# Sorted experts' weights as whole 8 KB rows of one expert, a gather buffer allocated a group later, and the residual added in the fourth group

## The chip, the core and the metric

One core of a Trainium2 chip runs the whole program. The metric is the device time of one execution in microseconds. The kernel before took 951.91 us (median of 3 runs, 950.81 to 952.39). The profiled execution took 952.46 us, of which 950.6 us lie between its first and its last instruction.

## What is computed

A trunk of two post-norm layers over 256 tokens of 1024 channels. Each layer has a token mixer (three attentions and their projections, which the change does not touch) and a mixture of 16 experts, of which every token uses two of one group of four:

```
x = layer_norm(x, ln_in_g, ln_in_b)
for l in range(2):
    mix = token_mixer(x, ...)
    x = layer_norm(ALPHA * x + mix, ln1_g[l], ln1_b[l])
    ffn = grouped_moe(x, router_w, router_bias, w_gate[l], w_up[l], w_down[l])
    x = layer_norm(ALPHA * x + ffn, ln2_g[l], ln2_b[l])

# grouped_moe, with combine (256 x 16) zero but for the two experts chosen per token
for e in range(16):
    hid = silu(t @ w_gate[e]) * (t @ w_up[e])       # w_gate, w_up: 1024 x 512
    out = out + combine[:, e:e+1] * (hid @ w_down[e])   # w_down: 512 x 1024
```

All weights are float32, 6 MB for an expert in a layer, and each is read once: 96 MB of experts per layer.

## The kernel before

**Order of the work.** TensorE, GpSimd and the DMA queue of SyncE (SP) run in the order in which the program is written; VectorE and ScalarE are ordered by a scheduler. A first pass over the program, without instructions, plans when buffers are held and dropped; a second pass writes it.

**Buffers.** SBUF holds 25 slots of 8 KB per partition (`NS = 25`). Activations take some (x, xT, the split copies xh and xl, y, the gather buffer B), and all weights go through the others: a weight tile is one slot, 1 MB, 2048 floats on each of 128 partitions. `weight(i)` asks for load number i, `drop(i)` gives its slot back, and after each drop `pump()` (L267) issues as many further loads as the plan leaves slots for. A load is a DMA on SP's queue. It waits for the last reader of its slot.

**The expert groups.** `build_stream` lists the loads of a layer: first the mixer's, then the experts in seven groups p = 0 to 6. Groups 0 and 1 are experts 0 to 3, two each. The other 12 experts are sorted on the chip by their number of tokens, so that which expert is loaded is known only when the sorting (`sort`, L1270) is done: the four smallest form group 2 ("four"), and groups 3 to 6 hold two each. Each group has the loads of w_gate, w_up and w_down, each in two halves h.

**What a weight tile holds before.** A half h of a weight is 128 rows (partitions) of 2048 floats. A tile of the kernel before holds one half of that half (`i`, 1024 floats, 4 KB per row) for two experts side by side. A sorted tile is loaded by two DMAs of 512 KB, one for each expert, since their numbers come from registers (L243 to 245). The four's half h is four tiles, a pair's is two.

**What a group computes.** In `moe`, tokens gathered for the experts of a group (xg) are multiplied with gate and up (L1488): for the four 128-row blocks rr of half h, one matmul of each expert in turn; each expert's outputs stand on their own rows of the PSUM bank. `done` (L1580) drops a tile after every second rr. Then follow Silu and product, the scatter of the group before (`scatter`, L1425 to 1429: its outputs are added to the sums R in PSUM by one-hot matrices), four transposes (L1512), and w_down (L1535), whose outputs go to y. The very last tile of the last group's w_down is loaded in four DMAs of 256 KB, so that its last piece is small.

**What else the change touches.** `seeds` (L1420) opens the sums R with the residual: eight matmuls of the split x with the identity, in group 1. `gather` (L1366) makes xg for the next four or the next two pairs; for pairs it needs a second buffer, `self.B`, which is allocated in the first call, in group 1.

Of the kernel before, what the change touches and what calls it, by code (L numbers as in the profile page):

```python
# [17 lines left out]
L, T, D, E, FF = 2, 256, 1024, 16, 512  # L18
KC = D // 128
# [111 lines left out]
class Kernel:  # L131
# [49 lines left out]
    def build_stream(self):  # L181
        self.loads = []
        self.units = []
        for l in range(L):
            off = 0
            for g, n, w in GROUPS:
                k = 0
                while k < n:
                    m = min(PER_SLOT[g], n - k)
                    sid = len(self.loads)  # L190
                    self.loads.append(("mix", l, off, m * w))
                    j = 0
                    while j < m:
                        u = min(PER_UNIT[g], m - j)
                        self.units.append(dict(l=l, g=g, k=k + j, n=u, w=w, slot=sid, o=j * w,
                                               last=(j + u == m)))
                        j += u
                    k += m
                    off += m * w
            self.moe_base = getattr(self, "moe_base", {})  # L200


            self.groups = [(0, 1), (2, 3)]
            if self.general:
                self.groups += [(e, e + 1) for e in range(4, E, 2)]
            else:
                self.groups += [tuple(range(E - QUAD, E))] + [(e, e + 1) for e in range(FIXED, E - QUAD, 2)]
            for p, g in enumerate(self.groups):
                self.moe_base[l, p] = len(self.loads)
                for nm in ("w_gate", "w_up", "w_down"):  # L210
                    for h in range(2):
                        for i in range(2):
                            for e in range(0, len(g), 2):
                                self.loads.append((nm, l, g[e], h, i))
        self.li = 0
        self.order, self.numbers = {}, {}
        self.wt = {}
        self.ui = 0
        self.si = 0
        self.split_tiles = {}  # L220
        self.used = []

    def load_next(self):
        d = self.loads[self.li]
        if d[0] == "mix":
            _, l, off, n = d
            t = self.S.new([128, 2048], F32, "w", weight=True)
            m = 672 if off == 0 else n
            for i in range(0, n, m):
                self.nc.sync.dma_start(t[:, i:i + m], self.a["w1"][l, :, off + i:off + i + m])  # L230
        else:
            nm, l, e, h, i = d
            t = self.S.new([128, 2048], F32, "w", weight=True)
            t2 = t.rearrange("p (i n) -> p i n", i=2)
            dma, w = self.nc.sync.dma_start, self.a[nm]
            if (nm, e, h) == ("w_gate", 0, 0):

                dma(t2, w[l, i, h].rearrange("i p n -> p i n"))
            elif self.sorted(d):

                n = 2 if nm == "w_down" and (e, h, i) == (self.groups[-1][0], 1, 1) else 1
                for k in range(n):
                    o = slice(k * 1024 // n, (k + 1) * 1024 // n)  # L243
                    for j in range(2):
                        dma(t2[:, j, o], w[l, bass.ds(self.number(l, e + j), 1), h, i, :, o].rearrange("e p n -> p (e n)"))
            else:
                dma(t2, w[l, e:e + 2, h, i].rearrange("e p n -> p e n"))
        self.wt[self.li] = t
        self.li += 1
        if self.li == self.LATE:  # L250
            self.late_loads()

    def sorted(self, d):

# [74 lines left out]
    WARM0 = (6, 0)  # L329
    LATE = 4  # L330
    DENSE = (1, 1, 5)
    BT = 2

    def unit(self, keep=False):
# [1079 lines left out]


    def seeds(self):
        self.R = [[self.psum([128, 512], "ab"[t]) for _ in range(2)] for t in range(2)]
# [7 lines left out]
    def scatter(self, oht, ys, t, js=(0, 1)):  # L1425
        lt = oht[:, t * 128:(t + 1) * 128]
        for j in js:
            for i in range(2):
                self.nc.tensor.matmul(self.R[t][j], lt, ys[:, i, j], start=False, stop=True, skip_group_check=True)

    def moe(self, l, last_layer):
        nc = self.nc
# [7 lines left out]
        p = 2  # L1440
# [4 lines left out]
        self.xg, self.bk, self.oh, self.ohr = {}, {}, {}, {}  # L1445
# [6 lines left out]
        first = self.gather_pair(0)  # L1452
# [3 lines left out]
        late = None  # L1456
        for p, es in enumerate(G):
            xg = self.xg[p]
            n = len(es)
# [19 lines left out]
            for which, h in ((0, 0), (1, 0), (0, 1), (1, 1)) if p == 0 else ((0, 0), (0, 1), (1, 0), (1, 1)):  # L1479
                ps = (pg, pu)[which]  # L1480
                known = p == 0 and which == 0 and h == 0
                i0 = wi + (4 * which + 2 * h) * n // 2
                for rr in range(4):
                    r = 4 * h + rr
# [1 line left out]
                        nc.tensor.matmul(ps[:64], self.oh[0][:, rr, 0], self.G[:, rr], start=rr == 0, stop=False)  # L1486
                    for e in range(int(known), n):
                        nc.tensor.matmul(ps[e * w:(e + 1) * w], xg[:, r, e * w:(e + 1) * w],  # L1488
                                         self.block(i0, n, rr, e, known), start=r == 0, stop=r == KC - 1)
                    self.done(i0, n, rr, known)  # L1490
# [22 lines left out]
            nc.scalar.activation(ht, ph, AF.Copy)  # L1513
            next(seeds, None)
            if p == 1:
                self.scatter(*late, 0)
            if late:
                self.scatter(*late, 1)
            if last:
                self.tail_rows()  # L1520
            self.steps(gath, ga[1])
# [8 lines left out]
                ysum = self.ts[:, 8:10]  # L1530
            for j in range(2):
                i0 = wi + (8 + 2 * j) * n // 2
                for c in range(4):
                    for e in range(n):
                        nc.tensor.matmul(py[j][e * w:(e + 1) * w], ht[:, c, e * w:(e + 1) * w],  # L1535
                                         self.block(i0, n, c, e), start=c == 0, stop=c == 3)
                    self.done(i0, n, c)
                self.pump()
                if j == 0:
                    self.steps(gath, 4)  # L1540
# [29 lines left out]
        if last_layer:  # L1570
            self.rest()

    def block(self, i, n, k, e, known=False):

        if known:
# [4 lines left out]
    def done(self, i, n, k, known=False):  # L1580

        if known and k == 3:
            self.drop(i + 1)
            self.pump()
        elif not known and k % 2:
            for j in range(n // 2):
                self.drop(i + k // 2 * n // 2 + j)
                self.pump()

    def steps(self, gen, n):  # L1590
        for _ in range(n):
# [76 lines left out]
    def overflow(self, l, hs):  # L1668
# [15 lines left out]
            nc.vector.tensor_tensor(xT[:, r], xT[:, r], pb[:, 2:].rearrange("p t n -> p (t n)"), op=OP.add)  # L1684

        def part(nm, e, h):
            nc.sync.dma_start(w[h].rearrange("p (i n) -> p i n", i=2), self.a[nm][l, e, h].rearrange("i p n -> p i n"))

        for e in range(E):
            for t in range(2):  # L1690
# [100 lines left out]
def _pack(x):  # L1791
# [51 lines left out]
    ke = lambda w: w.reshape(L, E, 2, 2, 2, 128, FF).transpose(0, 1, 2, 3, 5, 4, 6).reshape(L, E, 2, 2, 128, 1024)  # L1843
    kd = lambda w: w.reshape(L, E, 2, 2, 128, 2, 512).transpose(0, 1, 5, 2, 4, 3, 6).reshape(L, E, 2, 2, 128, 1024)
# [20 lines left out]
```

## Time and profile before

| | us |
|---|---|
| median of 3 runs | 951.91 (950.81 to 952.39) |
| profiled execution | 952.46 |
| its span, first to last instruction | 950.6 |
| TensorE busy in it | 905.7 (95%) |
| granted TensorE clock | 0.996 of full speed |

The two layers look alike. In the first, the mixer ends and routing begins near 251 us, the experts' matmuls run from 272.8 to 473.0 us, and the next layer's mixer begins at 479.6 us; in the second the experts run from 736.3 to 936.1 us. The busy share of TensorE stays near nine tenths in every stage, in the later expert groups too, where the waits named in the timeline are waits for weights: a matmul's busy time there includes standing behind one whose weights are late. So the share alone does not tell what binds; the chain that ended last and the releasers of the waits do.

### The profile page before, as it was taken

To read this page: it belongs to the slowest core of one execution; us is meant where nothing else is said; L and a number is where in the kernel's file an instruction comes from. 1 tells how busy PE (TensorE), PEld (TensorE's weight loads), DVE (VectorE), ACT (ScalarE), POOL (GpSimd) and SP (SyncE) were. 2 spreads that over 40 slices of the span, in tenths; PEclk is the share of its full clock that TensorE was granted. 3 is DMA by queue.
4 is the path that set the end of the run, shared out by engine and by line. 5 is a ranking of instruction groups with operands and counts; after the bars stand their busy time and mean duration, and the time that the engine had idled before them with its cause. 6 is when DMAs were issued, how large, how long until landed. Compare 5 with 4: busy or idle time off the path is not lost.

```text
span 950.6 us, 15321 instructions
## 1 busy us (share of the span) xinstructions
PE 905.7 (95%) x5835; PEld 624.5 (66%) x5835; DVE 425.1 (45%) x754; ACT 368.2 (39%) x724; POOL 295.5 (31%) x217
## 2 busy tenths in 40 slices
PE   5999999999999999999989999999999999999995
PEld 4999989899754543433379989889985443444322
DVE  6686666648741111100177765684686211111004
ACT  4586646563412111011256766566433111111003
POOL 4359646563300100010071977465622010000000
PEclk9999999999999999999999999999999999999998
DMA  9941263748879999999994407363978899999994
GB/s 342 377 157 67 79 255 110 290 166 322 309 273 351 410 404 409 409 401 409 405 415 188 175 2 263 114 250 112 347 264 331 317 364 390 409 409 409 401 410 153
DMA packets 68842, 277.22 MB, mean 292 GB/s; under 512 B 7428, under 2 KB 8068, under 8 KB 62852
## 3 DMA queue, kind: packets, MB, share of 16 engines
q1 hardware_dynamic: 68056, 272.88, 74.6%
q10 hardware_dynamic: 576, 3.15, 0.9%
q8 instruction: 48, 0.79, 0.3%
q14 instruction: 34, 0.28, 0.1%
q0 software_dynamic: 128, 0.13, 0.0%
HBM read 275.08 MB, written 1.05 MB: 290 GB/s over the span
## 4 chain that ended last, share of the span: by engine, by line
PE 60%; DMA 27%; DVE 6%; ACT 3%; POOL 2%; issue 2%; SPq 1%; ACTq 0%; POOLq 0%; DVEq 0%
DMA w<-in_w_up_dram 9%; DMA w<-in_w_gate_dram 9%; DMA w<-in_w_down_dram 9%; PE psa L736 8%; PE psa L738 7%; PE psa L737 7%; PE psa L1488 7%; PE pss L1535 5%; PE psa L157 2%; PE psa L1014 2%; PE psb L992 2%; PE psa L158 2%; PE psa L159 2%; PE psa L1346 2%; PE pss L931 1%
## 5 line engine op out<-in xcount | busy, mean ns | idle before, releaser
L301 POOL TENSOR_TENSOR whl<-w,whl 128x1024 fp32r<-128x1024 f32 (+1 forms) x83 | 193.4, 2345 | 189.4 <-ACT whl L297 113.1
L297 ACT ACTIVATE whl<-w 128x1024 fp32r<-128x1024 f32 (+2 forms) x146 | 138.6, 967 | 70.1 <-PE psa L738 29.1
L1488 PE MATMUL psa<-w,xT 128*64 128x512 f32 (+1 forms) x752 | 145.7, 595 | 3.0 <-DMA w<-in_w_up_dram 3.0
L736 PE MATMUL psa<-xTh,whl 128*128 128x256 f32 x480 | 138.3, 288 | 1.6 <-DVE oT L1017 1.4
L737 PE MATMUL psa<-xTl,whl 128*128 128x256 f32 x480 | 135.7, 283 | 0.0
L738 PE MATMUL psa<-xTh,whl 128*128 128x256 f32 x480 | 135.6, 283 | 0.0
L1488 PEld LDWEIGHTS psa<-w,xT 128*64 128x64 f32 (+1 forms) x752 | 45.7, 127 | 99.7 <-issue 86.0
L1535 PE MATMUL pss<-w,xT 128*64 128x512 f32 (+1 forms) x512 | 100.1, 595 | 0.0
L736 PEld LDWEIGHTS psa<-xTh,whl 128*128 128x128 f32 x480 | 91.8, 191 | 8.5 <-issue 6.2
L1499 DVE TENSOR_TENSOR xT<-xT,psa 128x512 f32<-128x512 f32 x14 | 9.6, 687 | 195.3 <-PE psa L1488 195.3
L738 PEld LDWEIGHTS psa<-xTh,whl 128*128 128x128 f32 x480 | 91.9, 191 | 0.0
L737 PEld LDWEIGHTS psa<-xTl,whl 128*128 128x128 f32 x480 | 91.9, 191 | 0.0
L1488 PE MATMUL psa<-w,xg 128*64 128x512 f32 x256 | 72.8, 605 | 4.4 <-DMA w<-in_w_up_dram 2.7
L301 DVE TENSOR_TENSOR whl<-w,whl 128x768 fp32r<-128x768 f32 (+2 forms) x63 | 67.3, 1089 | 14.2 <-ACT whl L297 13.7
L1535 PEld LDWEIGHTS pss<-w,xT 128*64 128x64 f32 (+1 forms) x512 | 32.0, 130 | 54.3 <-issue 50.4
L477 POOL MEMSET lngb<- 128x2048 f32 x2 | 3.6, 1806 | 200.1 <-DMA w<-in_w_gate_dram 100.1
L1488 PEld LDWEIGHTS psa<-w,xg 128*64 128x64 f32 x256 | 22.0, 136 | 54.5 <-issue 23.6
L736 PE MATMUL psa<-oT,whl 128*128 128x256 f32 x192 | 55.3, 288 | 0.0
L1552 DVE SCALAR_TENSOR_TENSOR y<-pss,ws,y 128x512 fp32r<-128x512 f32 x26 | 19.5, 750 | 79.0 <-ACT y L1551 74.0
L737 PE MATMUL psa<-oT,whl 128*128 128x256 f32 x192 | 54.3, 283 | 0.0
L738 PE MATMUL psa<-oT,whl 128*128 128x256 f32 x192 | 54.3, 283 | 0.0
L1551 ACT ACTIVATE y<-pss,ws 128x512 fp32r<-128x512 f32 x26 | 17.8, 686 | 77.3 <-PE pss L1535 64.1
(346 smaller groups left out, 1669.4 us busy)
## 6 DMA issues: line engine op xcount, KB each, us to landing
w<-in_w_gate_dram SPq DMA_DIRECT2D x96, 512.0 KB, 10.1
w<-in_w_up_dram SPq DMA_DIRECT2D x96, 512.0 KB, 10.1
w<-in_w_dram SPq DMA_DIRECT2D x46, 1024.0 KB, 7.2
w<-in_w_down_dram SPq DMA_DIRECT2D x92, 512.0 KB, 10.1
w<-in_w_gate_dram SPq DMA_DIRECT2D x16, 1024.0 KB, 5.0
w<-in_w_up_dram SPq DMA_DIRECT2D x16, 1024.0 KB, 7.7
w<-in_w_down_dram SPq DMA_DIRECT2D x16, 1024.0 KB, 7.4
w<-in_w_dram SPq DMA_DIRECT2D x18, 768.0 KB, 13.3
```

Of the source, the lines that this page charges most:

```text
L157: mm(out, lh, rh, start=start, stop=False, skip_group_check=skip)
L158: mm(out, ll, rh, start=False, stop=False, skip_group_check=skip)
L159: mm(out, lh, rl, start=False, stop=stop, skip_group_check=skip)
L297: self.nc.scalar.activation(hi[:, :n], raw, AF.Copy)
L301: e.tensor_tensor(lo[:, :n], raw, hi[:, :n].bitcast(F32), op=OP.subtract)
L736: mm(out, wh, xh, start=start, stop=False, skip_group_check=True)
L737: mm(out, wh, xl, start=False, stop=False, skip_group_check=True)
L738: mm(out, wl, xh, start=False, stop=stop, skip_group_check=True)
L992: nc.tensor.transpose(ps[:, kc, t * 128:(t + 1) * 128], P[:, t, j, kc * 128:(kc + 1) * 128], self.ident)
L1488: nc.tensor.matmul(ps[e * w:(e + 1) * w], xg[:, r, e * w:(e + 1) * w], self.block(i0, n, rr, e, known), start=r == 0, stop=r == KC - 1)
L1535: nc.tensor.matmul(py[j][e * w:(e + 1) * w], ht[:, c, e * w:(e + 1) * w], self.block(i0, n, c, e), start=c == 0, stop=c == 3)
L1552: nc.vector.scalar_tensor_tensor(ys[:, 1, j], py[j], ws, ys[:, 0, j].bitcast(F32), op0=OP.mult, op1=OP.subtract)
```

## The change

1. Weights of the experts lie in HBM as [layer, expert, half h, 128, 2048] instead of [layer, expert, h, i, 128, 1024] (an arrangement made on the host). For groups 2 to 6, a weight tile is now one expert's whole half h: one DMA of 1 MB with 8 KB rows. Only the last half of w_down in the last group keeps the old form (`whole`). Groups 0 and 1 keep it too, but for the first half of their w_gate, which held one expert per tile already and is now read in 8 KB rows.
2. `block` and `done` follow: a matmul of expert e reads the tile of e, and the tiles of a half are all dropped after its fourth block rr.
3. `self.B` is allocated by the first gather for pairs, in group 2.
4. R is opened by the first scatter, in group 1 (`first`), and the residual's eight matmuls are added in group 3 (`SEED = 3`).

```diff
@@ build_stream
                 for nm in ("w_gate", "w_up", "w_down"):
                     for h in range(2):
-                        for i in range(2):
-                            for e in range(0, len(g), 2):
-                                self.loads.append((nm, l, g[e], h, i))
+                        if self.whole(nm, p, h):
+                            self.loads += [(nm, l, e, h, None) for e in g]
+                        else:
+                            self.loads += [(nm, l, g[0], h, i) for i in range(2)]
@@ load_next
-            if (nm, e, h) == ("w_gate", 0, 0):
-
-                dma(t2, w[l, i, h].rearrange("i p n -> p i n"))
+            one = lambda e: w[l, bass.ds(self.number(l, e), 1), h].rearrange("e p n -> p (e n)") if self.sorted(d) else w[l, e, h]
+            if i is None:
+                dma(t, one(e))
             elif self.sorted(d):
...
                     for j in range(2):
-                        dma(t2[:, j, o], w[l, bass.ds(self.number(l, e + j), 1), h, i, :, o].rearrange("e p n -> p (e n)"))
+                        dma(t2[:, j, o], one(e + j)[:, i * 1024 + o.start:i * 1024 + o.stop])
             else:
-                dma(t2, w[l, e:e + 2, h, i].rearrange("e p n -> p e n"))
+                dma(t2, w[l, e:e + 2, h, :, i * 1024:(i + 1) * 1024].rearrange("e p n -> p e n"))
...
+    def whole(self, nm, p, h):
+
+
+        if (nm, p, h) == ("w_gate", 0, 0):
+            return True
+        return not self.general and p > 1 and (nm, p, h) != ("w_down", len(self.groups) - 1, 1)
@@ gather
-        if p == 2:
+        n = 1 if four else 2
+        if n == 2 and self.B is None:
 
             self.B = self.S.new([128, 2, KC, 128], F32, "xg")
-            self.places = self.xg[0], self.B[:, 0]
-        n = 1 if four else 2
-        dst = self.places[:n]
+        dst = (self.xg[0], self.B[:, 0]) if n == 2 else (self.xg[0],)
@@ seeds, scatter
-                self.nc.tensor.matmul(self.R[t][j], self.idr, self.xh[:, t, cs], start=True, stop=False)
-                self.nc.tensor.matmul(self.R[t][j], self.idr, self.xl[:, t, cs], start=False, stop=True)
+                self.nc.tensor.matmul(self.R[t][j], self.idr, self.xh[:, t, cs], start=False, stop=True, skip_group_check=True)
+                self.nc.tensor.matmul(self.R[t][j], self.idr, self.xl[:, t, cs], start=False, stop=True, skip_group_check=True)
...
-                self.nc.tensor.matmul(self.R[t][j], lt, ys[:, i, j], start=False, stop=True, skip_group_check=True)
+                self.nc.tensor.matmul(self.R[t][j], lt, ys[:, i, j], start=first and i == 0, stop=True, skip_group_check=True)
@@ moe
-            seeds = self.seeds() if p == 1 else iter(())
+            seeds = self.seeds() if p == self.SEED else iter(())
+            if p == 1:
+                self.R = [[self.psum([128, 512], "ab"[t]) for _ in range(2)] for t in range(2)]
@@ block, done
-        o = (e % 2 * 2 + k % 2) * 512
-        return self.weight(i + k // 2 * n // 2 + e // 2)[:, o:o + 512]
+        o = (e * 2 + k % 2) * 512
+        return self.weight(i + k // 2)[:, o:o + 512]
...
+        for j in (es if k == 3 else ()) if whole else (k // 2,) if k % 2 else ():
+            self.drop(i + j)
             self.pump()
```

On SP's queue, at the first sorted loads of the first layer (w_gate of the four; `sord` is the sorted order, from which an expert's number is read into a register), the kernel before has:

```order
L245 DMA w_2929<-in_w_gate_dram 128x1024
L263 TENSOR_LOAD sord_2908
L263 ISA x2
L245 ISA
L245 DMA w_2929<-in_w_gate_dram 128x1024
L263 TENSOR_LOAD sord_2908
L263 ISA x2
L245 ISA
L245 DMA w_2956<-in_w_gate_dram 128x1024
```

The same place on SP's queue in the changed kernel:

```order
L239 DMA w_2929<-in_w_gate_dram 128x2048
L270 TENSOR_LOAD sord_2908
L270 ISA x2
L239 ISA
L239 DMA w_2945<-in_w_gate_dram 128x2048
L270 TENSOR_LOAD sord_2908
L270 ISA x2
L239 ISA
L239 DMA w_2971<-in_w_gate_dram 128x2048
```

Each tile is filled by one DMA instead of two, and the second expert has a tile of its own.

On TensorE, the two halves of w_up in the last group of the first layer, before (each row is one tile with its four matmuls, two blocks rr by two experts; the trace shows each matmul as two instructions; psa_4012 is up's sum, psa_3164 a quarter of R):

```order
L1488 MATMUL psa_4012<-w_3854,xg_3172 64x512 x4
L1488 MATMUL psa_4012<-w_3861,xg_3172 64x512 x4
L1488 MATMUL psa_4012<-w_3870,xg_3172 64x512 x4
L1488 MATMUL psa_4012<-w_3873,xg_3172 64x512 x4
L1429 MATMUL psa_3164<-y_3982,oht_3962 128x512 x2
```

And in the changed kernel the second of these halves:

```order
L1495 MATMUL psa_3942<-w_3808,xg_3378 64x512
L1495 MATMUL psa_3942<-w_3810,xg_3378 64x512
L1495 MATMUL psa_3942<-w_3808,xg_3378 64x512
L1495 MATMUL psa_3942<-w_3810,xg_3378 64x512
L1495 MATMUL psa_3942<-w_3808,xg_3378 64x512
L1495 MATMUL psa_3942<-w_3810,xg_3378 64x512
L1495 MATMUL psa_3942<-w_3808,xg_3378 64x512
L1495 MATMUL psa_3942<-w_3810,xg_3378 64x512
```

The matmuls and their order of experts are the same; they now change between two tiles, the first expert's (w_3808) and the second's (w_3810), and the second matmul already needs the later tile.

On TensorE in group 3 of the changed kernel, where gate and up have ended (psa_3150, psa_3151, psb_3152 are quarters of R, xh and xl the split residual):

```order
L1495 MATMUL psa_3509<-w_3347,xT_2651 64x512
L1427 MATMUL psa_3150<-xh_3116,idr_80 128x512
L1428 MATMUL psa_3150<-xl_3117,idr_80 128x512
L1427 MATMUL psa_3151<-xh_3116,idr_80 128x512
L1428 MATMUL psa_3151<-xl_3117,idr_80 128x512
L1435 MATMUL psa_3150<-y_3435,oht_3017 128x512 x2
L1435 MATMUL psa_3151<-y_3435,oht_3017 128x512 x2
L1521 MATMUL pss_3588<-idr_80,xT_2651 128x128 x4
L1427 MATMUL psb_3152<-xh_3116,idr_80 128x512
L1428 MATMUL psb_3152<-xl_3117,idr_80 128x512
```

The eight residual matmuls (four are shown before the transposes) stood at the same place of group 1 before, ahead of the scatter.

## Rows read from the trace of the kernel before

**Rows 1.** The profile's page: span and busy time; GB/s in 40 slices of the span.

```profile
span 950.6 us, 15321 instructions
...
PE 905.7 (95%) x5835; PEld 624.5 (66%) x5835; DVE 425.1 (45%) x754; ACT 368.2 (39%) x724; POOL 295.5 (31%) x217
...
GB/s 342 377 157 67 79 255 110 290 166 322 309 273 351 410 404 409 409 401 409 405 415 188 175 2 263 114 250 112 347 264 331 317 364 390 409 409 409 401 410 153
```

**Rows 2.** Chain that ended last, first layer: start us, us, what.

```profile
336.44 10.23 DMA w<-in_w_down_dram
...
451.18 10.22 DMA w<-in_w_up_dram
...
461.45 1.93 PE psa L1488 x6
...
465.89 7.09 PE pss L1535 x32
```

**Rows 3.** The same chain, second layer.

```profile
914.26 10.22 DMA w<-in_w_up_dram
...
924.53 1.93 PE psa L1488 x6
```

**Rows 4.** Timeline of TensorE: start, us, instruction, [idle before it <- releaser].

```profile
382.81 9.80 PE L1488 MATMUL psa<-w,xg 128*64 128x512 f32 x42
392.82 2.35 PE L1488 MATMUL psa<-w,xg 128*64 128x512 f32 x8 [0.21 <-DMA w<-in_w_up_dram]
...
400.47 1.20 PE L1429 MATMUL psa<-y,oht 128*128 128x512 f32 x4
...
413.62 7.89 PE L1488 MATMUL psa<-w,xT 128*64 128x512 f32 x34
...
431.90 1.19 PE L1429 MATMUL psa<-y,oht 128*128 128x512 f32 x4
```

**Rows 5.** The same timeline, the last group of the first layer.

```profile
442.34 3.54 PE L1488 MATMUL psa<-w,xg 128*64 128x512 f32 x10
...
463.31 1.20 PE L1429 MATMUL psa<-y,oht 128*128 128x512 f32 x4
```

**Rows 6.** Timeline of SP's DMA issues.

```profile
277.13 18.71 SPq L245 DMA_DIRECT2D w<-in_w_gate_dram  x16
300.55 15.41 SPq L245 DMA_DIRECT2D w<-in_w_up_dram  x16
```

**Rows 7.** Busy time by stretch: PE, PEld, DVE, ACT, POOL; PEclk, DMA share, GB/s.

```profile
300.00:307.00 7.00, 7.00 (x36) 2.35 (x34) 0.75 (x1) 0.69 (x1) 0.00 (x0) 1.00 0.73 238
307.00:331.00 24.00, 24.00 (x144) 12.35 (x140) 2.95 (x6) 4.81 (x8) 4.67 (x2) 1.00 1.02 408
```

**Rows 8.** The same by other stretches; from 499 on only 8 KB rows arrive.

```profile
493.50:504.50 11.00, 11.00 (x70) 10.34 (x69) 7.29 (x18) 5.20 (x13) 4.30 (x8) 1.00 1.02 421
499.00:506.00 7.00, 7.00 (x45) 6.20 (x44) 5.23 (x15) 2.97 (x8) 1.81 (x4) 1.00 1.02 425
...
346.69:451.18 104.49, 101.65 (x525) 42.75 (x524) 12.38 (x22) 13.73 (x25) 2.48 (x2) 1.00 1.03 407
```

**Rows 9.** Chain in the second group, 300 to 336 us: start us, us, what.

```profile
302.22 13.73 PE psa L1488 x64
315.96 0.43 PE psa L1421
316.39 0.23 PE psa L1422
...
331.55 1.92 PE psa L1488 x16
333.48 0.29 SPq L245
```

**Rows 10.** What SP's queue waited for, 296 to 336 us: us, times, longest.

```profile
SPq L245 <- PE pss L1535: 6.5, 3, 4.5
SPq L245 <- PE psa L1402: 4.6, 1, 4.6
```

More of the change, by code (lines that the diff above doesn't have):

```diff
@@ L235, in load_next @@
             dma, w = self.nc.sync.dma_start, self.a[nm]
-            if (nm, e, h) == ("w_gate", 0, 0):
-                dma(t2, w[l, i, h].rearrange("i p n -> p i n"))
+            one = lambda e: w[l, bass.ds(self.number(l, e), 1), h].rearrange("e p n -> p (e n)") if self.sorted(d) else w[l, e, h]
+            if i is None:
+                dma(t, one(e))
             elif self.sorted(d):
-                n = 2 if nm == "w_down" and (e, h, i) == (self.groups[-1][0], 1, 1) else 1
-                for k in range(n):
-                    o = slice(k * 1024 // n, (k + 1) * 1024 // n)
+                for k in range(1 + i):
+                    o = slice(k * 1024 // (1 + i), (k + 1) * 1024 // (1 + i))
                     for j in range(2):
-                        dma(t2[:, j, o], w[l, bass.ds(self.number(l, e + j), 1), h, i, :, o].rearrange("e p n -> p (e n)"))
+                        dma(t2[:, j, o], one(e + j)[:, i * 1024 + o.start:i * 1024 + o.stop])
             else:
-                dma(t2, w[l, e:e + 2, h, i].rearrange("e p n -> p e n"))
+                dma(t2, w[l, e:e + 2, h, :, i * 1024:(i + 1) * 1024].rearrange("e p n -> p e n"))
         self.wt[self.li] = t
@@ L331 @@
     DENSE = (1, 1, 5)
+    SEED = 3
     BT = 2
@@ L1416, in seeds @@
     def seeds(self):
-        self.R = [[self.psum([128, 512], "ab"[t]) for _ in range(2)] for t in range(2)]
         for t in range(2):
@@ L1420, in seeds, with scatter @@
                 cs = slice(j * 512, (j + 1) * 512)
-                self.nc.tensor.matmul(self.R[t][j], self.idr, self.xh[:, t, cs], start=True, stop=False)
-                self.nc.tensor.matmul(self.R[t][j], self.idr, self.xl[:, t, cs], start=False, stop=True)
+                self.nc.tensor.matmul(self.R[t][j], self.idr, self.xh[:, t, cs], start=False, stop=True, skip_group_check=True)
+                self.nc.tensor.matmul(self.R[t][j], self.idr, self.xl[:, t, cs], start=False, stop=True, skip_group_check=True)
             yield
-    def scatter(self, oht, ys, t, js=(0, 1)):
+    def scatter(self, oht, ys, t, js=(0, 1), first=False):
         lt = oht[:, t * 128:(t + 1) * 128]
@@ L1444, in moe @@
         end = max(fours)
-        self.xg, self.bk, self.oh, self.ohr = {}, {}, {}, {}
+        self.xg, self.bk, self.oh, self.ohr, self.B = {}, {}, {}, {}, None
         self.one_hot(0, fours[0], False)
@@ L1481, in moe @@
                 known = p == 0 and which == 0 and h == 0
+                whole = self.whole(("w_gate", "w_up")[which], p, h)
                 i0 = wi + (4 * which + 2 * h) * n // 2
@@ L1488, in moe @@
                         nc.tensor.matmul(ps[e * w:(e + 1) * w], xg[:, r, e * w:(e + 1) * w],
-                                         self.block(i0, n, rr, e, known), start=r == 0, stop=r == KC - 1)
-                    self.done(i0, n, rr, known)
+                                         self.block(i0, whole, rr, e), start=r == 0, stop=r == KC - 1)
+                    self.done(i0, whole, rr, range(int(known), n))
                     if p == 0 and (which, h, rr) == self.GP:
@@ L1515, in moe @@
             if p == 1:
-                self.scatter(*late, 0)
+                self.scatter(*late, 0, first=True)
             if late:
-                self.scatter(*late, 1)
+                self.scatter(*late, 1, first=p == 1)
             if last:
@@ L1532, in moe @@
                 i0 = wi + (8 + 2 * j) * n // 2
+                whole = self.whole("w_down", p, j)
                 for c in range(4):
@@ L1535, in moe @@
                         nc.tensor.matmul(py[j][e * w:(e + 1) * w], ht[:, c, e * w:(e + 1) * w],
-                                         self.block(i0, n, c, e), start=c == 0, stop=c == 3)
-                    self.done(i0, n, c)
+                                         self.block(i0, whole, c, e), start=c == 0, stop=c == 3)
+                    self.done(i0, whole, c, range(n))
                 self.pump()
@@ L1571, in moe, with block, done @@
             self.rest()
-    def block(self, i, n, k, e, known=False):
-        if known:
+    def block(self, i, whole, k, e):
+        if whole:
             return self.weight(i + e)[:, k * 512:(k + 1) * 512]
-        o = (e % 2 * 2 + k % 2) * 512
-        return self.weight(i + k // 2 * n // 2 + e // 2)[:, o:o + 512]
-    def done(self, i, n, k, known=False):
-        if known and k == 3:
-            self.drop(i + 1)
+        o = (e * 2 + k % 2) * 512
+        return self.weight(i + k // 2)[:, o:o + 512]
+    def done(self, i, whole, k, es):
+        for j in (es if k == 3 else ()) if whole else (k // 2,) if k % 2 else ():
+            self.drop(i + j)
             self.pump()
[L1585 to L1588, printed above, removed]
     def steps(self, gen, n):
@@ L1686, in part @@
         def part(nm, e, h):
-            nc.sync.dma_start(w[h].rearrange("p (i n) -> p i n", i=2), self.a[nm][l, e, h].rearrange("i p n -> p i n"))
+            nc.sync.dma_start(w[h], self.a[nm][l, e, h])
         for e in range(E):
@@ L1841, in _pack @@
     bias = tab[idx][:, :, pairs].transpose(0, 2, 1).reshape(128, 2, 4, 384)
-    ke = lambda w: w.reshape(L, E, 2, 2, 2, 128, FF).transpose(0, 1, 2, 3, 5, 4, 6).reshape(L, E, 2, 2, 128, 1024)
-    kd = lambda w: w.reshape(L, E, 2, 2, 128, 2, 512).transpose(0, 1, 5, 2, 4, 3, 6).reshape(L, E, 2, 2, 128, 1024)
+    ke = lambda w: w.reshape(L, E, 2, 4, 128, FF).transpose(0, 1, 2, 4, 3, 5).reshape(L, E, 2, 128, 2048)
+    kd = lambda w: w.reshape(L, E, 4, 128, 2, 512).transpose(0, 1, 4, 3, 2, 5).reshape(L, E, 2, 128, 2048)
     ew = {n: ke(x[n]) for n in ("w_gate", "w_up")}
```

## The prediction

> **What bounds the kernel now.** I read the busy table first, then the GB/s by slices, then the chain that ended last, then the timelines of TensorE and SP around the places the chain names. TensorE is busy 95% of the span [rows 1], which would make the change, a matter of transfers, worthless. But the GB/s row shows two plateaus of 401 to 415, the 14th to 21st slice and the 35th to 39th, the later expert groups of the two layers; elsewhere the rate goes up and down. The chain says the same: in the first layer it runs through twelve DMA hops without a gap, the first at 336.44 us and the last ending at 461.40 [rows 2], then through TensorE to the layer's end; in the second layer likewise, up to 924.48 [rows 3]. A hop is one DMA from issue to landing, and the next is issued when it has landed: a hop of 10.22 us stands for eight DMAs of 512 KB (4.19 MB, 410 GB/s). TensorE is its own bound until about 392 us; from there it waits for DMAs, first with 0.21 us at 392.82 [rows 4]. So the later experts' stage ends when the stream of weights ends, and a stage's gain is what shortens the stream or the work behind its end.
>
> When does that stream begin? At 300 to 307 us the DMAs are 73% busy, from 307 to 331 102% at 408 GB/s [rows 7], and the slices that follow keep that rate. Before 307 SP waits for slots which TensorE has to give back: 4.5 us at a w_down of group 0 [rows 10]. A faster transfer gains nothing there.
>
> **Part 1: 8 KB rows.** SP issues 16 DMAs of 512 KB, eight sorted tiles, from 277.13 and goes on at 300.55 [rows 6]. Of a layer's 72 sorted tiles (12 experts, 6 each) 64 remain, and the last four (w_down of the last group) land after the up tile on which the chain leaves the stream: 60 tiles count. Price before: a hop of 10.22 us is four tiles, 2.555 us for 1.0486 MB. Price after: the trace of before has 8 KB rows in the mixer's prefetch. From 499 to 506 us, where only such rows arrive, the rate is 425 GB/s, from 493.5 to 504.5, with some 6 KB rows, 421 [rows 8]: 2.467 and 2.491 us a tile. The gain is 0.088 or 0.064 us a tile; against the stretch of 407 GB/s [rows 8] (2.576 us), which holds the small disturbances of a long stream, it is up to 0.109. I take 0.08, between the first two and nearer to the stretch of 8 KB rows alone: 60 x 0.08 = 4.8 us a layer, ends 3.8 and 6.5.
>
> The Trainium skill, DMA: Bandwidth & Descriptors, section Bandwidth, has it that a load from HBM is held by the HBM's share of a core, about 358 GB/s, so that the form of a row would not matter. This trace does not agree: 407 and 425 GB/s were moved. By that rule the 4.8 us would be 0; the price of this stands with the rivals.
>
> **Part 2: what TensorE still has to do when the last up tile lands.** Before, the last DMA brings a half tile of the second expert, two of its four blocks, and six instructions follow it, 1.93 us [rows 2, 3]. After, the last DMA brings all four blocks. The second matmul in the order needs that tile, so the first expert's later blocks stand behind it: 14 instructions follow, 8 more. In a stretch without waits 64 instructions take 13.73 us [rows 9], 0.2145 us each: 8 x 0.2145 = 1.72 us. Nothing hides it: silu, scatter, transposes and w_down stand behind it on TensorE, and w_down runs its 32 instructions in 7.09 us without a gap [rows 2], so it is TensorE's time and not the landing of w_down that counts there. w_down's first half also needs two tiles at once, 2 x 2.48 = 5.0 us behind the last up tile; TensorE is there at about 1.93 + 1.72 + 2.5 (461.45 + 1.93 to 465.89) = 6.2 us, so no wait is added. Ends: 0, if the first expert's instructions slip ahead, and 3.4, if w_down pays the same once more.
>
> At the other ends of halves the same 1.72 us fall into TensorE's slack. Gate and up take 13.73 us; they last 17.65 us in group 4 (382.81 to 400.47), 18.28 in group 5 (413.62 to 431.90) [rows 4] and 20.97 in group 6 (442.34 to 463.31) [rows 5]: 3.9, 4.6 and 7.2 us of waits, 15.7 in all, against a stream that ends 4.8 us earlier. That leaves group 4 about at balance and groups 5 and 6 still waiting, so the stream stays the bound.
>
> **Part 3: slots, B and the residual.** Whole tiles come back later: the four's first tiles after 32 instructions instead of 16. SP got the slot it waited for at 333.48, after 16 instructions of 1.92 us [rows 9]; now after some 3.8. Against that, the eight residual matmuls leave group 1: the first 0.43, the others 0.23 us [rows 9], 2.0 us in all, so that TensorE is at the four 2.0 us earlier, and four tiles come back at once. B's slot is free for one more weight tile from 317 to 346 us, 2.5 us more of queued stream, where SP had waited 4.6 us [rows 10]. The three cancel within some tenths, and the queue, full at 408 GB/s through this stretch [rows 7], hides the rest: 0, with ends of -1 and +1 us a layer. In group 3 the 2.0 us come back on TensorE, which the next groups' slack takes. SP issues half as many sorted DMAs; it is not the bound while its queue is full: 0. The 8 KB rows of the first w_gate lie in group 0, where slots decide: 0.
>
> **Sum.** 4.8 - 1.72 = 3.1 us a layer, 6.2 us in two. From the profiled execution, 952.46 us (its span of 950.6 and 1.9 around it): 946.3. That execution lies 0.55 above the median of the runs, so I predict 945.8 us.
>
> **Rivals.**
> (a) More than this: the stream also starts better. In 300 to 307 the DMAs stood idle for about 7 x 0.28 = 2.0 us [rows 7], when each slot was filled by two DMAs in turn; one DMA per slot and a freed slot could fill that. 945.8 - 2 x 2.0 = 941.8 us. For it: fewer issues per slot. Against: the waits there are for TensorE [rows 10], and B's slot is free only later.
> (b) Less: TensorE becomes the bound before the last group. Group 4 is about at balance, and the 1.72 us of each half could be paid before the stream can make up for it; half the stream's gain goes: 945.8 + 2 x 2.4 = 950.6 us. Against: 4.6 and 7.2 us of waits in the last two groups [rows 4, 5].
> (c) The row's form does not matter, and only the later start of the last half remains: 951.9 + 2 x 1.72 = 955.3 us. For it: the two rates compared come from different stages, and the windows of 8 KB rows are 7 to 11 us short. Against: 425 and 421 stand above every long stretch of 4 KB rows. This is what the skill's rule above would give.
> (d) Slower: the coarser tile is paid in each of the five groups with whole tiles, at each last half: 5 x 1.72 = 8.6 us a layer, 951.9 - 9.6 + 17.2 = 959.5 us. It decides once TensorE has no slack at a group's end, so that each late half pushes the next group. For it: TensorE never waits before 392. Against: up to there all tiles lie ready, and after it 15.7 us of waits a layer can take it up. The Trainium skill, Perfetto Trace Analysis, section DMA Optimizations, says that smaller pieces let work start sooner; here it holds at the last half, where I charge it.
>
> **Numbers.** Forecast (943.5 to 948.5) 0.62, (a) 0.14, (b) 0.14, (c) 0.06, (d) 0.04. About 0.2%, 1.9 us, is what a measurement of this kernel tells from no change: faster is below 950.0, slower above 953.8. Faster: 0.62 + 0.14 + 0.05 of (b) = 0.81; slower: (c) and (d), 0.10; same: the 0.09 left of (b). The unknown sizes (2 x 3.8 - 2 x 1.72 up to 2 x 6.5 - 2 x 1.72, and 1 us a layer of part 3) reach from 940.9 to 949.7 around the sum; with part of (a) and (b) the range is 941.5 to 950.5.
>
> **What would show it.** In the profile after: the expert stage's plateaus at 420 to 425 GB/s; hops of one 1 MB DMA each, eight of them in flight, about 2.48 us a tile; 14 TensorE instructions, about 3.6 us, between the last up landing and the scatter; the first layer's w_down ending near 469.9 instead of 472.98, the second's 6.2 us earlier than before; residual matmuls in group 3; no dip in the DMA share after 307. Wrong if the plateaus stay at 407 to 410 (c), if TensorE has no wait for DMAs left in groups 5 and 6 (b, d), or if the stream is dense before 307 (a).

## The result, and the profile after

The changed kernel takes 946.36 us (median of 4 runs, 946.20 to 946.77) against 952.15 us (4 runs, 950.81 to 953.20): ratio 0.9941, 95% interval 0.9923 to 0.9958, 5.8 us less. The forecast was 945.8, its range 941.5 to 950.5. Beside the experiments the same kernel was timed twice more: 948.01 against 953.05 (ratio 0.9950, 0.9938 to 0.9963) and 947.81 against 952.75 (0.9943, 0.9929 to 0.9957). So the gain is 4.9 to 5.8 us by the three pairs of medians, and the sum of 6.2 lies above all three.

The page of the changed kernel: span and busy time, and GB/s in 40 slices [rows 1].

```profile
span 944.7 us, 14890 instructions
...
PE 890.5 (94%) x5835; PEld 622.1 (66%) x5835; DVE 425.8 (45%) x754; ACT 368.3 (39%) x724; POOL 293.1 (31%) x217
...
GB/s 343 381 170 54 83 252 110 292 162 325 303 275 365 402 421 421 421 413 421 410 417 151 170 5 278 98 250 110 351 261 331 326 352 422 420 421 421 412 419 97
```

Both plateaus stand at 410 to 422 (15th to 21st slice and 34th to 39th) where they stood at 401 to 415; the 14th slice, at 402, stands below its 410 of before. TensorE has the same number of instructions, yet 15 us less of it count as busy: the busy share of 95%, from which one would have called it the bound, is no measure of its work: it includes standing behind late weights.

The chain that ended last at the end of layer 1, and in layer 2 (start us, us, what) [rows 2, 3]:

```profile
435.74 19.78 DMA w<-in_w_up_dram
455.57 3.65 PE psa L1495 x14
459.21 1.14 PE psa L1435 x4
...
461.73 7.09 PE pss L1545 x32
468.82 0.67 PE psa L1435 x2
...
896.09 19.76 DMA w<-in_w_up_dram
...
915.89 3.65 PE psa L1495 x14
```

A hop is now one 1 MB DMA that was issued when seven others were still ahead of it: 19.78 / 8 = 2.47 us a tile, where it was 2.555. Fourteen TensorE instructions, 3.65 us together, follow the last up tile instead of six in 1.93. To read such a chain: in the full stream a new DMA is issued when the one eight before it has landed (here at 435.74, after a landing at 435.62), with seven still in flight; a hop's start is no pause of the stream. From 345 to 450 us SP waits 77 us for such landings and 2.4 us for TensorE.

TensorE's timeline in groups 4, 5 and 6, the last three of layer 1 (what waits, and for what) [rows 4, 5]:

```profile
389.92 3.65 PE L1495 MATMUL psa<-w,xg 128*64 128x512 f32 x16 [0.21 <-DMA w<-in_w_up_dram]
394.77 3.65 PE L1495 MATMUL psa<-w,xg 128*64 128x512 f32 x14 [1.19 <-DMA w<-in_w_up_dram]
...
420.76 3.65 PE L1495 MATMUL psa<-w,xT 128*64 128x512 f32 x16 [1.38 <-DMA w<-in_w_up_dram]
425.74 3.65 PE L1495 MATMUL psa<-w,xT 128*64 128x512 f32 x14 [1.32 <-DMA w<-in_w_up_dram]
...
450.59 3.65 PE L1495 MATMUL psa<-w,xg 128*64 128x512 f32 x16 [1.30 <-DMA w<-in_w_up_dram]
455.57 3.65 PE L1495 MATMUL psa<-w,xg 128*64 128x512 f32 x14 [1.32 <-DMA w<-in_w_up_dram]
```

TensorE still waits for DMAs in groups 4, 5 and 6, so it did not become the bound.

Windows of the changed kernel (busy us and count of PE, PEld, DVE, ACT, POOL; PEclk, DMA share, GB/s) [rows 7, 8], and what SP's queue waited for from 296 to 336 us [rows 10]:

```profile
300.00:307.00 7.00, 7.00 (x34) 2.30 (x32) 0.75 (x1) 1.27 (x2) 0.00 (x0) 1.00 0.91 310
307.00:316.00 9.00, 9.00 (x48) 3.56 (x45) 0.69 (x1) 1.90 (x3) 4.67 (x2) 1.00 0.95 376
316.00:330.00 14.00, 14.00 (x102) 7.45 (x105) 2.77 (x6) 3.01 (x6) 0.00 (x0) 1.00 1.01 418
330.00:345.00 15.00, 15.00 (x137) 5.91 (x130) 0.94 (x2) 0.84 (x2) 0.00 (x0) 1.00 1.02 423
345.00:392.00 47.00, 46.79 (x274) 20.41 (x274) 6.15 (x11) 6.93 (x13) 0.00 (x0) 1.00 1.01 421
...
SPq L239 <- PE pss L1545: 13.7, 5, 5.0
SPq L239 <- PE psa L1495: 12.1, 6, 4.6
SPq L239 <- PE psb L1435: 3.7, 1, 3.7
```

SP's waits in this stretch are longer than before (30.3 us in all, before 21.7), and from 316 us on the stream runs at 418 GB/s and more nevertheless; each of SP's issues now brings 1 MB.

**Where the time went.** To compare executions I count from the same TensorE instruction in each: the stage of layer 1 from a matmul in group 0 (287.6 us before) to the first tail row after w_down, the stage of layer 2 from the router likewise. Against the profile before: layer 1 -3.15 us, the mixer between +0.02, layer 2 -2.79. The program's start (-1.0) and its end (+1.0) cancel. Two more profiles of the changed kernel give -3.72 and -2.43, -3.25 and -2.89: about 0.3 us is what such a number is worth.

Inside a stage, the packets' records show when the weights' queue has moved the same number of bytes as before (us, minus is earlier; the first column is the time before):

```
layer 1       changed   rows alone   4 KB rows   slots alone   residual, no B
322.6 us       -0.09      -0.37        -0.39       +0.12          -0.16
337.6          -0.94      +0.37        -0.81       -0.38          -0.86
377.6          -2.04      -0.32        -0.72       -0.28          -1.96
417.6          -3.12      -1.47        -0.69       -0.28          -3.09
461.6          -4.38      -2.69        -0.70       -0.29          -4.39
layer 2
806.4          -1.49      +0.48        -0.93       -1.12          -1.49
846.4          -2.50      -0.69        -0.85       -1.10          -2.56
924.4          -4.76      -2.91        -0.85       -1.10          -4.76
```

The other columns are experiments, below (rows alone: 1; slots alone: 2; 4 KB rows: 3; "residual, no B", which has B early as before: 4). The changed kernel gains 1 to 1.5 us around the start of the full stream (some 335 us, and 800 in layer 2), and from there 2.8 us per 100 us, steadily.

### The profile page after: what moved, and what is told of

Its sections match the earlier page's. It is cut to its first block, busy times and chain, and to the rows that moved or that the text cites. A ratio compares the mean times of both kernels' runs of the same rounds, so it can differ in the third digit from the quotient of the medians.

```text
span 944.7 us, 14890 instructions
## 1 busy us (share of the span) xinstructions
PE 890.5 (94%) x5835; PEld 622.1 (66%) x5835; DVE 425.8 (45%) x754; ACT 368.3 (39%) x724; POOL 293.1 (31%) x217
## 3 DMA queue, kind: packets, MB, share of 16 engines
q10 hardware_dynamic: 576, 3.15, 0.9%
HBM read 275.08 MB, written 1.05 MB: 292 GB/s over the span
## 4 chain that ended last, share of the span: by engine, by line
PE 67%; DMA 19%; DVE 6%; ACT 3%; POOL 2%; issue 1%; SPq 0%; ACTq 0%; POOLq 0%; DVEq 0%
PE psa L1495 11%; DMA w<-in_w_up_dram 8%; PE psa L744 8%; PE psa L746 8%; PE psa L745 7%; DMA w<-in_w_down_dram 6%; PE pss L1545 6%; DMA w<-in_w_gate_dram 4%; PE psa L157 2%; PE psa L1022 2%; PE psb L1000 2%; PE psa L158 2%; PE psa L159 2%; PE psa L1354 2%; PE pss L939 1%
## 5 line engine op out<-in xcount | busy, mean ns | idle before, releaser
L1495 PE MATMUL psa<-w,xT 128*64 128x512 f32 (+1 forms) x752 | 142.3, 594 | 5.6 <-DMA w<-in_w_up_dram 5.6
L1495 PE MATMUL psa<-w,xg 128*64 128x512 f32 x256 | 61.4, 597 | 10.6 <-DMA w<-in_w_up_dram 8.0
L1495 PEld LDWEIGHTS psa<-w,xg 128*64 128x64 f32 x256 | 19.9, 136 | 51.4 <-issue 29.4
```

## The experiments

Each kernel ran beside the kernel before on the same chip; ratios are against that. Diffs are against the changed kernel unless said.

**1. Whole rows alone** (B allocated early and the residual in group 1, as before):

```
-    SEED = 3
+    SEED = 1
...
-        if n == 2 and self.B is None:
+        if p == 2:
...
```

> The changed kernel with B allocated in group 1 and the residual opened in group 1 as before: whole 8 KB rows alone. Theory (8 KB rows speed up the stream by about 0.08 us a tile, the last up half costs 1.72 us a layer, slots and residual are worth nothing): 946.4 us, within 1 us of the changed kernel. Rival (the freed slot and the earlier TensorE in group 2 start the stream better, up to 2 us a layer): 948 to 950.5 us, with dips in the DMA share between 310 and 345 us.

951.37 us, ratio 0.9994 (0.9984 to 1.0004): no gain clear of noise, and less than even the rival expected. The reading "the other two edits are worth nothing" falls. Its stages are -1.05 and -0.74. Its windows, and what SP waited for:

```profile
316.00:330.00 14.00, 14.00 (x99) 8.93 (x99) 2.48 (x6) 2.33 (x5) 0.00 (x0) 1.00 0.98 398
330.00:345.00 15.00, 15.00 (x135) 4.38 (x132) 0.75 (x1) 1.29 (x2) 0.00 (x0) 1.00 1.00 383
345.00:392.00 47.00, 45.45 (x270) 20.00 (x269) 6.84 (x12) 6.77 (x13) 0.00 (x0) 1.00 1.01 422
...
SPq L239 <- PE psb L1435: 5.5, 1, 5.5
```

After 345 us it moves 422 GB/s like the changed kernel; between 316 and 345 its queue runs dry, at 398 and 383 GB/s against 418 and 423. Whole tiles come back later, and SP waits for a slot meanwhile, for the scatter (L1435) 5.5 us where the changed kernel waits 3.7. By the table it stands 1.3 us behind the changed kernel at 337.6 and 2.0 at 806.4, and 1.7 and 1.85 at the ends.

**2. B and the residual alone**, with the tiles and rows of before (the kernel before, with the edits on B, `seeds` and `scatter`):

> The kernel before with only the later B and the residual in group 3; tiles and 4 KB rows as before. Theory: no change, 952.1 us within 1 us. Rival (slots and residual carry part of the gain): 948 to 950.5 us.

951.63 us, ratio 0.9996 (0.9987 to 1.0005), as expected. Small pieces of it can be seen: its table column gains 0.3 and 1.1 us, since the kernel before had dips too, 400 GB/s from 330 to 345 us and 379 from 792 to 807, which here are 409 and 408. The kernel before:

```profile
330.00:345.00 15.00, 15.00 (x136) 4.34 (x132) 0.75 (x1) 1.28 (x2) 0.00 (x0) 1.00 1.02 400
...
792.00:807.00 15.00, 15.00 (x128) 4.43 (x128) 1.76 (x4) 1.28 (x2) 0.00 (x0) 1.00 1.00 379
```

Taken alone neither part of the change moves the median; together they do. Which of the two edits fills these dips at the old tiles was not run.

**3. The changed kernel with 4 KB rows**, one DMA of 1 MB a tile (the weights lie in HBM as before):

```
-    one = lambda e: w[l, bass.ds(self.number(l, e), 1), h].rearrange("e p n -> p (e n)") if ...
+    one = lambda e: w[l, bass.ds(self.number(l, e), 1), h].rearrange("e i p n -> p (e i) n") if ...
...
```

> The changed kernel with the weights in HBM as before, so that a whole tile is still one DMA of 1 MB but of two 4 KB rows per partition. Theory (the length of a row sets the rate): the stream runs at 407 to 411 GB/s as before and the coarser last half still costs 1.72 us a layer: 954.5 to 955.5 us, slower than before. Rival (the number or size of the DMAs sets the rate): 946.4 us as the changed kernel, 420 GB/s.

954.65 us, ratio 1.0027 (1.0011 to 1.0042). Number and size of the DMAs are the changed kernel's, and the rate is that of before:

```profile
345.00:392.00 47.00, 45.26 (x266) 20.56 (x266) 6.14 (x11) 6.92 (x13) 0.00 (x0) 1.00 1.03 409
```

So the length of a row makes the rate. The packets' records agree: from 346 us to about 450 a 4 KB packet takes 162 ns in the median (kernel before), an 8 KB packet 313 (changed kernel); two short ones cost 11 ns more than a long one, and with 128 rows on 16 engines, eight long packets each, that is 0.09 us a tile, where the hops give 2.555 - 2.47 = 0.08. The DMAs' share is above 1.00 in both, so that share does not tell the two apart. Where the chain leaves the stream in layer 1 and layer 2:

```profile
458.82 3.65 PE psa L1495 x14
...
922.73 3.65 PE psa L1495 x14
```

Counted from the stage's same instruction these are 3.25 and 3.58 us later than in the changed kernel, and 1.63 and 0.92 earlier than before: the first pair is what 8 KB rows bring, the second what whole tiles and the other two edits bring together. By bytes, in the table's last rows, the parts are 3.7 and 3.9, and 0.7 and 0.85. A landing and a count of bytes can differ so, and two profiles of the same changed kernel stand 0.7 us apart in the row of 461.6 us: the parts are known to some tenths of a microsecond.

**4. Which of the other two edits?** The changed kernel again, then with the residual back in group 1 (`SEED = 1`), then with B early (`if p == 2:`).

> The changed kernel as it is, beside the three others: 946.3 us, ratio 0.994.

> Whole rows and the later allocation of B; the residual back in group 1. With both old places (the run with rows alone) SP waited for slots between 316 and 345 us and each layer lost some 2.1 us of the stream. If it is the one more slot of weights between 317 and 346 us that keeps the queue full, this kernel is where the changed one is, 946.3 to 947.5 us, and no slice of the expert stage goes below 415 GB/s. If it is TensorE reaching the four of group 2 by 2.0 us earlier, this kernel is where rows alone were, 950 to 951.4. If each gives half, 948.5.

> Whole rows and the residual in group 3; B allocated early as before. The mirror of the run with the later B alone: 950 to 951.4 us if the slot is what counts, 946.3 to 947.5 if the 2.0 us of TensorE in group 1 are, 948.5 if each gives half.

948.01 us (0.9950); with the later B but the residual in group 1, 951.75 (0.9991, 0.9982 to 1.0000); with the residual in group 3 and B early, 946.58 (0.9943, 0.9931 to 0.9955). As far as these runs can tell, it is the residual's move, all of it. TensorE's timeline of the changed kernel (gate and up of group 1, then its w_down):

```profile
301.05 13.90 PE L1495 MATMUL psa<-w,xT 128*64 128x512 f32 x64
...
320.87 3.65 PE L1545 MATMUL pss<-w,xT 128*64 128x512 f32 x16
```

and of the kernel with the residual in group 1, with its window from 330 us:

```profile
300.82 13.90 PE L1495 MATMUL psa<-w,xT 128*64 128x512 f32 x64
314.65 0.50 PE L1427 MATMUL psa<-xh,idr 128*128 128x512 f32 x1
...
322.46 3.65 PE L1545 MATMUL pss<-w,xT 128*64 128x512 f32 x16
...
330.00:345.00 15.00, 15.00 (x134) 4.81 (x133) 1.35 (x2) 1.29 (x2) 0.00 (x0) 1.00 0.97 371
```

From gate to w_down 19.82 us in the one and 21.64 in the other: 1.82 us later, and with it every slot that w_down and the four give back. SP's wait for the scatter (L1435) from 296 to 336 us is 5.5 us in both kernels with 8 KB rows and the residual in group 1, and 3.7 in both with it in group 3. The stream pays just that: 371 instead of 423 GB/s for 15 us are 15 x 52 / 421 = 1.85 us. With the residual in group 3 and B early the window is full without the slot that B lends:

```profile
330.00:345.00 15.00, 15.00 (x136) 5.19 (x129) 1.44 (x2) 1.06 (x2) 0.00 (x0) 1.00 1.01 420
```

In the table its column is the changed kernel's to 0.1 us from 337.6 on. The slot is lent from 317 to 346 us and then taken back. With the residual in group 1 the late B moves the dip (421 GB/s from 316 to 330 us and 371 from 330 to 345, against 398 and 383 with B early); it does not fill it.

**5. The tail.** The last half of w_up in half tiles of 512 KB, as before:

```
-                for k in range(1 + i):
-                    o = slice(k * 1024 // (1 + i), (k + 1) * 1024 // (1 + i))
+                n = 1 + i if nm == "w_down" else 1
+                for k in range(n):
+                    o = slice(k * 1024 // n, (k + 1) * 1024 // n)
...
-        return not self.general and p > 1 and (nm, p, h) != ("w_down", len(self.groups) - 1, 1)
+        return not self.general and p > 1 and (p, h) != (len(self.groups) - 1, 1) or nm == "w_gate" and p > 1 and not self.general
```

> The changed kernel, with the last half of w_up in the last group loaded as before: two tiles of two experts' half halves, each in two DMAs of 512 KB with 4 KB rows. Theory: six TensorE instructions instead of 14 follow the last up landing, 1.72 us a layer less, and two tiles pay 0.08 us each again: 946.4 - 2 x (1.72 - 0.16) = 943.3 us; w_down's last piece lands some tenths before it is needed. Rival (w_down's landing, not TensorE, ends the layer, so that the tail is hidden): 946.4 to 946.7 us, with a wait of TensorE for w_down.

> The last half of w_up in half tiles (512 KB) again, now beside the changed kernel itself. Its profile ended layer 1 by 1.7 and layer 2 by 1.3 us earlier than the changed one's, 3.0 us in all; its median was only 0.4 below. If the profile is right, 3.0 us below the changed kernel timed beside it (943 to 945 us, ratio 0.991 to 0.992); if the gain is lost elsewhere, the same as the changed kernel, ratio 0.994 to 0.995.

> The changed kernel once more, beside the three others: 946 to 948 us, ratio 0.994 to 0.995.

945.92 us (0.9940, 0.9925 to 0.9954); again, 945.68 (0.9927, 0.9915 to 0.9938) with the changed kernel beside it at 947.81 (0.9943). Its stages are -4.84 and -4.05, then -4.55 and -3.45. Against the mean of the changed kernel's three profiles (-3.37, -2.70) that is 1.2 to 1.5 us in layer 1 and 0.75 to 1.35 in layer 2, under the 1.56 of the theory. The timeline (second run) shows why:

```profile
446.04 3.65 PE L1496 MATMUL psa<-w,xg 128*64 128x512 f32 x16 [1.32 <-DMA w<-in_w_gate_dram]
451.04 7.08 PE L1496 MATMUL psa<-w,xg 128*64 128x512 f32 x30 [1.35 <-DMA w<-in_w_up_dram]
...
460.63 7.58 PE L1546 MATMUL pss<-w,xT 128*64 128x512 f32 x32
```

TensorE waits for the last whole tile of the first half, at 451.04, and then runs 30 instructions through the fine half without a wait: the end of the half before binds now. And w_down takes 7.58 us instead of 7.09: it has come up to its own landings (its first instruction starts at 460.63, a tile of w_down lands at 461.08, and the second starts at 461.11).

With the last line of that edit alone: of the half's two tiles the first comes in pieces of 512 KB, the second in pieces of a quarter tile (256 KB):

> The changed kernel with the last half of w_up in pieces of a quarter tile (256 KB), so that only 2 or 3 TensorE instructions need what lands last. By the theory of the tail (0.2145 us for each of the 14 instructions behind the last landing), some 11 instructions or 2.4 us a layer leave the tail; but w_down's landing then binds (with half-tile pieces it already cost 0.5 us of TensorE's wait in w_down), so 1.5 to 2.0 us a layer remain: 942.3 to 943.3 us against 946.3. If the tail is not what counts there, 946.3.

944.09 us (0.9915, 0.9902 to 0.9928), the lowest median of all, 3.9 us below the changed kernel timed beside it (948.01). But its profile doesn't support the step from 512 to 256 KB: the stages are -4.20 and -3.84, no better than with half tiles, and the chain has the same 30 instructions from the same place:

```profile
450.55 7.08 PE psa L1495 x30
...
460.13 7.74 PE pss L1545 x32
```

I take both fine forms as one, 2.1 and 3.9 us below the changed kernel where it was timed beside them; the two were not timed side by side, and all three medians lie above what was expected.

Half tiles with B early:

> The two pieces that paid, whole rows and the residual in group 3, with B allocated early as before, and the last half of w_up in half tiles. If the later B is worth nothing once the residual is moved, this is the same as the kernel with the fine last half and the later B, 943 to 945 us (ratio 0.991 to 0.992). If the later B holds part of the gain, it is 1 to 2 us slower than that.

946.89 us (0.9935, 0.9923 to 0.9947), stages -4.24 and -3.57. Its interval and that of the kernel with the later B (0.9915 to 0.9938) overlap: a difference in B is not shown.

**6. 8 KB rows in DMAs of 64 partitions**, two of 512 KB a tile:

```
-                dma(t, one(e))
+                for o in (slice(0, 64), slice(64, 128)):
+                    dma(t[o], one(e)[o])
```

> The changed kernel's tiles and 8 KB rows, each tile by two DMAs of 64 partitions and 512 KB instead of one of 1 MB. If the length of a row sets the rate, its plateaus stay at 419 to 422 GB/s and its time where the changed kernel's is; if the size of a DMA does, or if the number of issues costs something, they fall to 407 to 410 and it takes 4 to 5 us more a layer, 954 to 957 us. A DMA of 64 partitions could also use fewer of the 16 DMA engines at a time; then the rate would fall below 407.

1248.44 us, ratio 1.310 (1.307 to 1.312). It was meant to part the row's length from the DMA's size and says nothing on that (experiment 3 does), since something larger comes in. Its DMA share and GB/s by slices:

```profile
DMA  9623375779999999999994062777899999999995
GB/s 361 257 102 135 154 251 207 289 287 218 219 222 220 222 222 224 222 224 225 280 418 147 37 253 74 233 295 276 258 222 223 223 228 226 224 224 225 225 225 147
```

All sixteen DMA engines are busy, and move 222 GB/s, half of 421: an 8 KB packet takes 586 ns in the median of the whole run instead of 311. The Trainium skill, SBUF — State Buffer, section "Can I just issue two DMAs to hit both halves?", has it that only a transfer over all 128 partitions reaches all ports, and that two over the halves run one after the other. The measured half of the rate agrees; by which mechanism the packets become slow, no run here shows.

## Why the prediction was right, point by point

**The sum.** Per layer it was 4.8 - 1.72 = 3.1 us. Measured from the same instruction, the last up tile lands 4.88 us earlier in layer 1 and 4.50 in layer 2; less 1.72 that gives 3.16 and 2.78, and the stages are 3.15 and 2.79 shorter. The sum holds. How the 4.8 is made up does not, and that the total still came out is luck.

**Part 1, 8 KB rows: the rate right, the count wrong.** 2.47 us a tile and 419 to 423 GB/s over long stretches are what the short windows of [rows 8] promised. "60 tiles count" is the step that failed. It took the stream for the bound from 307 us on, because the DMAs were 102% busy there [rows 7]. But SP was still waiting for TensorE's slots, until 333.48 us, a row that I had [rows 9]; a faster row only waits longer for its slot there. In the table the steady gain begins at about 335 us: (461.5 - 335) / 2.555 = 49.5 tiles. Changed against 4 KB rows says the same: 0.30 us behind at 322.6, 0.13 ahead at 337.6 and 1.32 at 377.6. Experiment 3 gives 3.25 and 3.58 us for the rows by the landing, 0.066 to 0.073 us for each tile (layer 2 from some 800: 49 tiles), and 3.7 and 3.9 by bytes, 0.07 to 0.08 for each. The term predicted 4.8 with ends of 3.8 and 6.5; measured it is at its lower end or below.

**Part 2, the tail: right.** 14 instructions and 3.65 us, 1.72 more, in both layers. It is paid once a layer; the half tiles of experiment 5 give 1.2 to 1.5 us of it back in layer 1 and 0.75 to 1.35 in layer 2.

**Part 3: "the three cancel within some tenths" failed, by about what part 1 lacked.** Whole tiles coming back later put the stream behind the kernel before by 0.4 us at 337.6 and 0.5 at 806.4 (rows alone, in the table); I had charged 1.9. The residual's 2.0 us were worth nearly their length: between rows alone and the residual moved without B the ends of the table differ by 1.70 and 1.85. B's slot, put at up to 2.5, gave nothing. And the queue that I called full was read to 331 us only: the kernel before fell to 400 GB/s from 330 to 345 and to 379 in the same place of layer 2, and B and the residual together fill that too (experiment 2). Together, by the last up tile of experiment 3, 1.63 and 0.92 us of gain a layer (by bytes 0.7 and 0.85) where I wrote 0 with ends of -1 and +1. So 3.25 + 1.63 = 4.88 and 3.58 + 0.92 = 4.50: two errors of opposite sign in a total that came out.

**The rivals.** (a) fell: from 300 to 307 us the share rose from 0.73 to 0.91, but from 307 to 316 it is 0.95, where the kernel before has 1.02, and by 322.6 us the changed kernel is only 0.09 us ahead (table). In the kernel with B early the share from 300 to 307 is 0.80 with the same end: earlier bytes there were worth nothing. (b) fell: TensorE's waits in groups 4 to 6 remain. (c) fell by 421 against 409 GB/s. Nor does the share of some 358 GB/s, to which the Trainium skill (DMA: Bandwidth & Descriptors, section Bandwidth) holds a load from HBM, agree with either rate; the same section gives that share for two cores that stream at once and 425 GB/s, measured over 16 MB, for one alone, and this program runs on one core. (d) fell: the landing's gain less a single 1.72 us is the stage's gain, so nothing was paid at the ends of halves before the last.

**What I had said would show it.** The first layer's w_down ends at 461.73 + 7.09 = 468.82 (said: near 469.9, before 472.98) and the second's at 929.13, 6.9 us earlier than before (said: 6.2); 1.0 us of each is the program's earlier start. The residual runs in group 3, at 369.67 to 373 us. One sign did not come: from 307 to 316 us the DMA share has a dip, 0.95 and 376 GB/s where the kernel before has 1.02 and 406. None of the signs could have told 60 tiles from 50.

**A sum that does not come out.** The unknown sizes were said to reach from 940.9 to 949.7; the terms as given, 7.6 - 3.44 - 2 and 13 - 3.44 + 2 us off 951.9, reach from 940.3 to 949.7. The range stated holds either way.

## What to carry to other kernels

DMAs that are 100% busy don't yet make the stream the bound (here the share was 1.02 from 307 to 331 us): as long as the queue's issuer waits for slots, the engine that frees them can be, so count what a faster transfer brings only from the last such wait (here 333.48 us). When tiles are made larger, look for work that stands ahead of their release: moving it behind was worth its whole length here, 1.8 us of matmuls for 1.7 to 1.9 us of stream, and without it the better transfer gained nothing clear of noise. Try the last piece of a stream small (2 to 4 us here), and keep every DMA over all partitions (222 against 421 GB/s here).

## What the runs showed that I had not expected

Beside the halved rate of experiment 6: in layer 2's mixer some executions lose 1.5 us to TensorE's clock. Two profiles of the very same changed kernel, in windows from 480 us, first one without:

```profile
480.00:482.00 2.00, 0.63 (x4) 0.42 (x4) 1.18 (x1) 0.78 (x2) 0.63 (x1) 1.00 1.03 406
482.00:484.00 2.00, 1.20 (x6) 0.94 (x7) 1.29 (x2) 0.95 (x2) 1.94 (x3) 1.00 1.06 432
484.00:486.00 2.00, 2.00 (x15) 2.00 (x15) 0.85 (x1) 0.77 (x1) 2.00 (x7) 1.00 0.97 399
```

and one with it:

```profile
480.00:482.00 2.00, 0.62 (x7) 0.41 (x4) 1.47 (x1) 0.50 (x1) 0.92 (x1) 1.00 1.03 405
482.00:484.00 2.00, 1.16 (x5) 0.66 (x4) 1.22 (x2) 1.24 (x3) 1.66 (x2) 0.86 1.04 421
484.00:486.00 2.00, 2.00 (x8) 2.00 (x8) 0.07 (x1) 0.65 (x1) 2.00 (x9) 0.50 1.01 416
```

TensorE, which waits for VectorE's norm here, was busy 1.83 of the 4 us up to 484 in the one and 1.78 in the other. The granted clock stays at 1.00 (2.4 GHz) in the first; in the second it falls before 484 us (0.86 over 482 to 484) and is 0.50 (1.2 GHz) after, and the mixer ends 1.5 us later (947.07 and 948.54 us for the two executions). Of eleven profiles of kernels with whole tiles and 128 partitions five have it, whatever the edit, the one with 256 KB pieces among them. What decides it stays open; 1.5 us is nearly what the medians of the changed kernel differ by (946.4 to 948.0), so for an edit of 1 us the stages were the better measure.
